# A decoder trunk on one core: the pre-norm gain in x's transposes or in the projection's weights

## The chip, the cores and the metric

The kernel runs on one core of a Trainium2 chip. The metric is the device time of one execution in microseconds (us); a shorter time is better. The kernel before takes 1954.34 us, the median of three runs (1953.93 to 1958.12).

The engines named below: PE is TensorE, DVE is VectorE, ACT is ScalarE, POOL is GpSimd, SP is SyncE, which here issues the loads. Each engine takes its own queue of instructions in order.

## The reference: what is computed

Two decoder layers on x of 256 tokens by 2048 features, float32. Each layer is a normalised attention and a normalised squared-ReLU MLP, with a norm ahead of each and one behind:

```python
def rmsnorm(x, g):
    xf = x.astype(jnp.float32)
    y = xf * lax.rsqrt(jnp.mean(xf * xf, axis=-1, keepdims=True) + RMS_EPS)
    return (y * g.astype(jnp.float32)).astype(x.dtype)

def sq_relu_mlp(x, w_up, w_down):
    h = jax.nn.relu(x @ w_up)
    return (h * h) @ w_down
```

What counts here is `rmsnorm(x, g) @ w`. It is the sum over features k of x[t,k] g[k] w[k,n], times a factor of token t alone, which the kernel applies behind the product. The gain g[k] of a feature may stand with x or with w. Layer 0 has one gain ahead of its query, key and value projections (w_qkv_a); layer 1 has two on the same x, one for the shared keys and values (w_kv_shared) and one for the queries (w_q_b). Each MLP has one, ahead of w_up.

## The kernel before

Features are split into 16 k-blocks of 128, tokens into two halves of 128 (hf). Each product is made from three matmuls, since every float32 operand is held as a rounded part, hi, and the rest, lo: hi by hi, hi by lo, lo by hi.

`weights` makes one weight tile: SP loads 512 KB, which are two k-blocks by 512 columns (raw, three buffers), ACT casts it to hi and DVE subtracts hi from raw to give lo (six buffers each). With a gain it does so per k-block, 128x512 at a time, scaled by a column of gcol (L130 and L131); without one, in one piece of 128x1024 (L124 and L125). gcol holds the gains with features across partitions: `load_gains` brings gains in by a DMA, transposes them on PE (tile gps) and copies them to gcol on DVE (L98), the gain of the first attention first and the other four later.

`to_T` turns x: for a half hf and a group c of four k-blocks, four PE transposes (L184) go to one PSUM bank (pt), one ACT instruction casts the 512 columns to hi (L187), and one DVE instruction gives lo (L188). The tiles are called xa0 (for layer 0's attention; xa00 to xa03 by c), xm0 and xm1 (for the two MLPs) and xa1 (layer 1's attention), each with eight turns, 32 in all.

`head_proj` is the first product on a new turned x: it runs the first half over five weight tiles before the second half is needed (L200 to L202, accumulators kv0 and kv1). It serves the key and value projection of each layer and the first 512 columns of each MLP's w_up. `kv_evac` then brings the keys to SBUF (ktok, L235) and transposes them (pk, L243). `q_proj` makes the queries of one group, between which attention is computed; `up_feat` makes the other 512-column pieces of w_up (L508, L512); `col_pass` runs o_proj and w_down (L200 to L202 too). `add_normed` adds a normed output to x in four pieces of 512 columns (L173) and calls the turn of each piece behind it; with o_proj this is the seam into the MLP, with w_down that into the next layer's attention.

The program is written in the order of the computation. A scheduler of the build lays out each engine's queue before the run, by estimates of its own; at the start, the seams and in attention, instructions of several steps stand mixed on a queue. On the chip an engine waits at the head of its queue until what it needs is there.

## Time and profile before

| | before |
|---|---|
| median of three runs | 1954.34 us |
| the profiled execution | 1956.32 us |
| its span, first to last record | 1954.3 us |
| mean granted clock of PE | 0.997 of full |
| PE busy | 1928.2 us, 99% |
| DVE busy | 1273.6 us, 65% |
| ACT busy | 1097.2 us, 56% |

The durations are those of one profiled execution; 2.0 us of its time lie outside the span. "Busy" is the time that an engine had an instruction under way; matmul ends are modelled, and one instruction's row may run on past the start of the next on the same engine. [...]

### The profile page before, as it was taken

How to read it: one execution, taken by the hardware profiler on the slowest of the kernel's cores; microseconds unless marked ns; L12 is line 12 of the kernel's file. 1: busy time of each engine (PE TensorE's matmuls, PEld its weight loads, DVE VectorE, ACT ScalarE, POOL GpSimd, SP SyncE). 2: the span in 40 equal slices, each digit the busy share in tenths (PEclk: the TensorE clock that was granted, in tenths of full speed). 3: DMA queues.
4: the chain of work that ended last, by engine and by line, in shares of the span. 5: the costliest groups of instructions: out<-in, count | busy, mean ns of one | idle time of the engine just before them, and what ended most of it. 6: DMA issues, size and time to landing. Idle time of an engine off the chain costs nothing.

```text
span 1954.3 us, 28151 instructions
## 1 busy us (share of the span) xinstructions
PE 1928.2 (99%) x10318; PEld 1649.4 (84%) x10318; DVE 1273.6 (65%) x2177; ACT 1097.2 (56%) x1977; POOL 247.1 (13%) x306
## 2 busy tenths in 40 slices
PE   8999999999999999999999999999999999999998
PEld 7998788888888888888789988888888888888886
DVE  6898677546655664675578885775466556656654
ACT  7787566445544553554468874664455345435542
POOL 0242001000100110010202420010011002100111
PEclk9999999999999999999999999999999999999999
DMA  7534657666666666666554346566666666666663
GB/s 228 159 112 141 205 162 214 194 193 188 190 192 190 189 188 192 183 192 196 168 165 150 125 145 199 169 202 198 192 183 194 194 193 185 194 192 187 184 194 128
DMA packets 181642, 354.22 MB, mean 181 GB/s; under 512 B 10912, under 2 KB 11008, under 8 KB 180992
## 3 DMA queue, kind: packets, MB, share of 16 engines
q1 hardware_dynamic: 180736, 348.17, 59.4%
q10 hardware_dynamic: 736, 4.24, 0.6%
q8 instruction: 81, 1.33, 0.3%
q14 instruction: 57, 0.47, 0.1%
q0 software_dynamic: 32, 0.02, 0.0%
HBM read 350.28 MB, written 2.10 MB: 180 GB/s over the span
## 4 chain that ended last, share of the span: by engine, by line
PE 87%; DVE 5%; ACT 5%; DMA 2%; issue 1%; POOL 0%; DVEq 0%; ACTq 0%; SPq 0%
PE u L508 23%; PE o L200 15%; PE o L202 15%; PE o L201 14%; PE u L512 11%; ACT pr L338 1%; DVE lo L131 1%; DVE pr L325 1%; ACT hi L130 1%; PE kv L200 1%; PE kv L201 1%; PE kv L202 1%; PE q L271 1%; PE q L268 1%; PE q L270 1%
## 5 line engine op out<-in xcount | busy, mean ns | idle before, releaser
L131 DVE SCALAR_TENSOR_TENSOR lo<-raw,gcol,hi 128x512 fp32r<-128x512 f32 x672 | 485.9, 753 | 192.3 <-ACT hi L130 181.2
L125 DVE TENSOR_TENSOR lo<-raw,hi 128x1024 fp32r<-128x1024 f32 x320 | 394.5, 1234 | 330.9 <-ACT hi L124 330.3
L508 PE MATMUL u<-xm,hi 128*128 128x512 f32 x1920 | 603.5, 395 | 0.0
L130 ACT ACTIVATE hi<-raw,gcol 128x512 fp32r<-128x512 f32 x672 | 455.0, 716 | 244.4 <-PE u L508 96.3
L124 ACT ACTIVATE hi<-raw 128x1024 fp32r<-128x1024 f32 x320 | 338.9, 1059 | 403.5 <-PE o L202 321.5
L512 PEld LDWEIGHTS u<-xm,lo 128*128 128x128 f32 x1920 | 360.5, 188 | 84.9
L200 PE MATMUL o<-hi,h 128*128 128x512 f32 x1024 | 403.2, 394 | 0.0
L202 PE MATMUL o<-hi,h 128*128 128x512 f32 x1024 | 401.0, 392 | 0.0
L201 PE MATMUL o<-lo,h 128*128 128x512 f32 x1024 | 398.1, 389 | 0.0
L512 PE MATMUL u<-xm,lo 128*128 128x256 f32 x1920 | 377.9, 278 | 0.0
L508 PEld LDWEIGHTS u<-xm,hi 128*128 128x128 f32 x1920 | 293.0, 189 | 0.7
L519 POOL TENSOR_TENSOR us<-us,rb 128x256 f32<-128x256 f32 x120 | 116.0, 967 | 1257.3 <-DVE us L518 1257.3
L202 PEld LDWEIGHTS o<-hi,h 128*128 128x128 f32 x1024 | 192.2, 188 | 44.7
L201 PEld LDWEIGHTS o<-lo,h 128*128 128x128 f32 x1024 | 192.3, 188 | 42.1
L200 PEld LDWEIGHTS o<-hi,h 128*128 128x128 f32 x1024 | 192.5, 188 | 38.8
L268 PE MATMUL q<-xa,hi 128*128 128x256 f32 x512 | 147.0, 287 | 0.0
L271 PE MATMUL q<-xa,lo 128*128 128x256 f32 x512 | 144.8, 283 | 0.0
L270 PE MATMUL q<-xa,hi 128*128 128x256 f32 x512 | 144.4, 282 | 0.0
L521 ACT ACTIVATE h<-uh 128x256 fp32r<-128x256 f32 x120 | 50.2, 419 | 97.1 <-DVE uh L520 97.1
L200 PE MATMUL o<-hi,o 128*128 128x512 f32 x256 | 102.0, 398 | 0.0
L520 DVE SCALAR_TENSOR_TENSOR uh<-us 128x256 f32<-128x256 f32 x120 | 50.8, 423 | 77.5 <-POOL us L519 77.5
L202 PE MATMUL o<-hi,o 128*128 128x512 f32 x256 | 100.8, 394 | 0.4 <-POOL o L378 0.4
(116 smaller groups left out, 1909.3 us busy)
## 6 DMA issues: line engine op xcount, KB each, us to landing
raw<-in_w_up_dram SPq DMA_DIRECT2D x256, 512.0 KB, 4.1
raw<-in_w_down_dram SPq DMA_DIRECT2D x256, 512.0 KB, 4.2
raw<-in_w_qkv_a_dram SPq DMA_DIRECT2D x40, 512.0 KB, 4.1
raw<-in_w_o_a_dram SPq DMA_DIRECT2D x32, 512.0 KB, 4.2
raw<-in_w_q_b_dram SPq DMA_DIRECT2D x32, 512.0 KB, 3.8
raw<-in_w_o_b_dram SPq DMA_DIRECT2D x32, 512.0 KB, 4.1
raw<-in_w_kv_shared_dram SPq DMA_DIRECT2D x8, 512.0 KB, 3.6
x<-in_x_dram SPq DMA_DIRECT2D x8, 256.0 KB, 5.4
```

The source lines that it names most:

```text
L124: nc.scalar.activation(hi, raw, AF.Copy)
L125: nc.vector.tensor_sub(lo, raw, hi.bitcast(F32))
L130: nc.scalar.activation(hi[:, i], raw[:, i], AF.Copy, scale=g)
L131: nc.vector.scalar_tensor_tensor(lo[:, i], raw[:, i], g, hi[:, i].bitcast(F32), op0=ALU.mult, op1=ALU.subtract)
L200: nc.tensor.matmul(ps, xh, wh, start=first, stop=False)
L201: nc.tensor.matmul(ps, xh, wl, start=False, stop=False)
L202: nc.tensor.matmul(ps, xl, wh, start=False, stop=last)
L268: nc.tensor.matmul(o, hi[:, j, fs], t[:, :T], start=(k == 0 and f % 2 == 0), stop=False, skip_group_check=True)
L270: nc.tensor.matmul(o, hi[:, j, fs], t[:, T:], start=False, stop=False, skip_group_check=True)
L271: nc.tensor.matmul(o, lo[:, j, fs], t[:, :T], start=False, stop=(k == KT - 1), skip_group_check=True)
L508: nc.tensor.matmul(acc[f], hi[:, j, fs], xT[k // 4][:, k % 4], start=(k == 0), stop=False, skip_group_check=True)
L512: nc.tensor.matmul(acc[f][:, :T], lo[:, j, fs], xT[k // 4][:, k % 4, :T], start=False, stop=(k == KT - 1), skip_group_check=True)
```

## The change

`to_T` takes the index of a gain. With one, each turn is made in four pieces of 128 columns, one for each k-block: ACT casts a piece with the gain's column of gcol as its scale, and DVE multiplies the piece by the same column and subtracts hi. xa0 (gain 0), xm0 (gain 1) and xm1 (gain 4) have one: 24 of the 32 turns. The weight tiles of w_qkv_a (40) and of w_up (256) then have none and take the plain form of 128x1024; the 40 of w_kv_shared and w_q_b keep theirs, and xa1 is turned as before. Matmuls, loads and transposes are the same in number and shape. Lines behind `to_T` have numbers ten higher after the change.

```diff
-    def to_T(dst, name):
+    def to_T(dst, name, gi=None):
+
 
         def each(hf, c):
             if not dst:
@@ -184,8 +185,17 @@
                 nc.tensor.transpose(pt[:, j * P:(j + 1) * P], xs[hf][:, k * P:(k + 1) * P], ident)
             pt4 = pt.rearrange("p (j t) -> p j t", t=P)
             hi = dst[c][:, :, hf * P:(hf + 1) * P]
-            turned[0] = nc.scalar.activation(hi, pt4, AF.Copy).ins
-            nc.vector.tensor_sub(dst[c][:, :, T + hf * P:T + (hf + 1) * P], pt4, hi.bitcast(F32))
+            lo = dst[c][:, :, T + hf * P:T + (hf + 1) * P]
+            if gi is None:
+                turned[0] = nc.scalar.activation(hi, pt4, AF.Copy).ins
+                nc.vector.tensor_sub(lo, pt4, hi.bitcast(F32))
+                return
+            for j in range(4):
+                k = gi * KT + 4 * c + j
+                g = gcol[:, k:k + 1]
+                turned[0] = nc.scalar.activation(hi[:, j], pt4[:, j], AF.Copy, scale=g).ins
+                nc.vector.scalar_tensor_tensor(lo[:, j], pt4[:, j], g, hi[:, j].bitcast(F32),
+                                               op0=ALU.mult, op1=ALU.subtract)
         return each
 
     def act_tiles(tag, name):
@@ -213,14 +223,14 @@
         n = KT // 2
         head = []
         for i in range(min(STAG, n)):
-            head.append(weights(rows(w, 2 * i, 2, c0, 512), (2, 512), (gi, 2 * i)))
+            head.append(weights(rows(w, 2 * i, 2, c0, 512), (2, 512), gi and (gi, 2 * i)))
             step(0, i, head[i])
             if second and i == X1_AT:
                 second()
         for i, hl in enumerate(head):
             step(1, i, hl)
         for i in range(STAG, n):
-            hl = weights(rows(w, 2 * i, 2, c0, 512), (2, 512), (gi, 2 * i))
+            hl = weights(rows(w, 2 * i, 2, c0, 512), (2, 512), gi and (gi, 2 * i))
             for hf in range(NH):
                 step(hf, i, hl)
         return acc
@@ -257,7 +267,7 @@
 
         acc = [bank("a", f"q{i}") for i in range(2)]
         for i in range(KT // 2):
-            hi, lo = weights(rows(w, 2 * i, 2, g * 512, 512), (2, 512), (gi, 2 * i))
+            hi, lo = weights(rows(w, 2 * i, 2, g * 512, 512), (2, 512), gi and (gi, 2 * i))
             for j in range(2):
                 k = 2 * i + j
                 t = xT[k // 4][:, k % 4]
@@ -500,7 +510,7 @@
 
         acc = [bank(tag, f"u{f}") for f in range(4)]
         for i in range(KT // 2):
-            hi, lo = weights(rows(w, 2 * i, 2, c0, 512), (2, 512), (gi, 2 * i))
+            hi, lo = weights(rows(w, 2 * i, 2, c0, 512), (2, 512), gi and (gi, 2 * i))
             for f in range(4):
                 fs = slice(f * P, (f + 1) * P)
                 for j in range(2):
@@ -535,7 +545,7 @@
 
 
     xT = []
-    turn_x = to_T(xT, "xa0")
+    turn_x = to_T(xT, "xa0", 0)
     for c in range(4):
         turn_x(0, c)
 
@@ -545,7 +555,7 @@
         for c in range(4):
             turn_x(1, c)
 
-    layers = [(w_qkv_a[0], D, 0, w_qkv_a[0], 0, True, near, w_o_a[0]),
+    layers = [(w_qkv_a[0], D, None, w_qkv_a[0], None, True, near, w_o_a[0]),
               (w_kv_shared, 0, 2, w_q_b[0], 3, False, full, w_o_b[0])]
     for layer, (w_kv, c_kv, g_kv, w_q, g_q, with_sink, dist, w_o) in enumerate(layers):
         kv = head_proj(xT, w_kv, c_kv, g_kv, second_half if layer == 0 else None)
@@ -560,9 +570,9 @@
         for g in range(HKV):
             attention(g, q_proj(xT, w_q, g, g_q), ks, vs, oT, dist, with_sink, r, std)
         xT = []
-        o_proj(oT, w_o, n_attn_post[layer], to_T(xT, f"xm{layer}"))
+        o_proj(oT, w_o, n_attn_post[layer], to_T(xT, f"xm{layer}", 1 + 3 * layer))
         xm, xT = xT, []
-        mlp(xm, w_up[layer], w_down[layer], 1 + 3 * layer, n_mlp_post[layer], x_rstd,
+        mlp(xm, w_up[layer], w_down[layer], None, n_mlp_post[layer], x_rstd,
             to_T(xT, "xa1") if layer == 0 else store)
```

The order of the queues comes out another way. At the start on DVE (gcol is the table of gains, gps its transposes in PSUM, lo a weight tile's rest, pt0 to pt3 the turns' banks), before:

```order
L86 MEMSET eps_90 128x1
L98 COPY gcol_92<-gps_95 128x16
L131 SCALAR_TENSOR_TENSOR lo_145<-raw_143,gcol_92,hi_144 128x512
L188 TENSOR_TENSOR xa00_109<-pt0_113,xa00_109 128x4x128
L188 TENSOR_TENSOR xa01_110<-pt1_120,xa01_110 128x4x128
L188 TENSOR_TENSOR xa02_111<-pt2_127,xa02_111 128x4x128
L188 TENSOR_TENSOR xa03_112<-pt3_134,xa03_112 128x4x128
L131 SCALAR_TENSOR_TENSOR lo_145<-raw_143,gcol_92,hi_144 128x512
L131 SCALAR_TENSOR_TENSOR lo_159<-raw_157,gcol_92,hi_158 128x512 x2
```

and after:

```order
L86 MEMSET eps_90 128x1
L125 TENSOR_TENSOR lo_169<-raw_167,hi_168 128x1024
L125 TENSOR_TENSOR lo_181<-raw_179,hi_180 128x1024
L125 TENSOR_TENSOR lo_193<-raw_191,hi_192 128x1024
L98 COPY gcol_92<-gps_95 128x16
L197 SCALAR_TENSOR_TENSOR xa00_109<-pt0_113,gcol_92,xa00_109 128x128
L197 SCALAR_TENSOR_TENSOR xa01_110<-pt1_126,gcol_92,xa01_110 128x128
L197 SCALAR_TENSOR_TENSOR xa02_111<-pt2_139,gcol_92,xa02_111 128x128
L197 SCALAR_TENSOR_TENSOR xa00_109<-pt0_113,gcol_92,xa00_109 128x128
```

The copy of gcol moved from the head of the queue to behind three whole lo tiles, and the pieces of the first three turns stand interleaved behind it. The next lo tile (of lo_269) stands six rows further on, with the fourth piece of xa00 behind it. On ACT the hi casts of the first three tiles stand ahead of the first turn piece in the same way. PE's queue has the first matmul on xa00 behind the sixteen transposes of the first half, as before.

At the seam behind layer 0's o_proj on DVE (x0 is the first half of x, ug1 the output's second half, stat a norm's scalars, xm00 to xm03 the turned x), before:

```order
L173 SCALAR_TENSOR_TENSOR x0_62<-ug0_2186,stat_3051,x0_62 128x512 x4
L188 TENSOR_TENSOR xm00_3060<-pt0_3064,xm00_3060 128x4x128
L188 TENSOR_TENSOR xm01_3061<-pt1_3072,xm01_3061 128x4x128
L188 TENSOR_TENSOR xm02_3062<-pt2_3080,xm02_3062 128x4x128
L188 TENSOR_TENSOR xm03_3063<-pt3_3088,xm03_3063 128x4x128
L432 TENSOR_TENSOR ug1_2187<-o11_2786,grow_2184 128x512
L142 TENSOR_REDUCE stat_3131<-parts_2189 128x1
L131 SCALAR_TENSOR_TENSOR lo_3227<-raw_3225,gcol_92,hi_3226 128x512
L145 TENSOR_SCALAR stat_3131<-stat_3131 128x1
L131 SCALAR_TENSOR_TENSOR lo_3227<-raw_3225,gcol_92,hi_3226 128x512
L131 SCALAR_TENSOR_TENSOR lo_3241<-raw_3239,gcol_92,hi_3240 128x512 x2
```

and after, from the last instruction on ug1 (ahead of it stand the lo of the first four weight tiles, the four adds to x0, and the first pieces of xm00 and xm01):

```order
L442 TENSOR_TENSOR ug1_2155<-o11_2754,grow_2152 128x512
L197 SCALAR_TENSOR_TENSOR xm00_3028<-pt0_3032,gcol_92,xm00_3028 128x128
L197 SCALAR_TENSOR_TENSOR xm01_3029<-pt1_3046,gcol_92,xm01_3029 128x128
L197 SCALAR_TENSOR_TENSOR xm02_3030<-pt2_3060,gcol_92,xm02_3030 128x128
L197 SCALAR_TENSOR_TENSOR xm03_3031<-pt3_3074,gcol_92,xm03_3031 128x128
L142 TENSOR_REDUCE stat_3123<-parts_2157 128x1
L125 TENSOR_TENSOR lo_3249<-raw_3247,hi_3248 128x1024
L145 TENSOR_SCALAR stat_3123<-stat_3123 128x1
L125 TENSOR_TENSOR lo_3291<-raw_3289,hi_3290 128x1024
L197 SCALAR_TENSOR_TENSOR xm00_3028<-pt0_3032,gcol_92,xm00_3028 128x128
```

The lo of weight tile 4 moved to ahead of the adds, and the lo of tiles 5 and 6 (lo_3249, lo_3291) moved to between the second and the third piece of xm00. The fourth piece of xm00 stands four rows further on.

At the same place on ACT (o11 is an accumulator of o_proj, hi a weight tile's cast), before:

```order
L153 ACTIVATE junk_3128,parts_2189<-o11_2786 128x512
L187 ACTIVATE xm00_3060<-pt0_3064 128x4x128
L187 ACTIVATE xm01_3061<-pt1_3072 128x4x128
L130 ACTIVATE hi_3240<-raw_3239,gcol_92 128x512
L187 ACTIVATE xm02_3062<-pt2_3080 128x4x128
L187 ACTIVATE xm03_3063<-pt3_3088 128x4x128
L130 ACTIVATE hi_3240<-raw_3239,gcol_92 128x512
L130 ACTIVATE hi_3284<-raw_3283,gcol_92 128x512 x2
```

and after:

```order
L153 ACTIVATE junk_3120,parts_2157<-o11_2754 128x512
L124 ACTIVATE hi_3248<-raw_3247 128x1024
L196 ACTIVATE xm00_3028<-pt0_3032,gcol_92 128x128
L196 ACTIVATE xm01_3029<-pt1_3046,gcol_92 128x128
L124 ACTIVATE hi_3290<-raw_3289 128x1024
L196 ACTIVATE xm00_3028<-pt0_3032,gcol_92 128x128
L196 ACTIVATE xm01_3029<-pt1_3046,gcol_92 128x128
L196 ACTIVATE xm02_3030<-pt2_3060,gcol_92 128x128
L196 ACTIVATE xm03_3031<-pt3_3074,gcol_92 128x128
L536 DMA grow_3187<-in_norm_mlp_post_dram 128x2048
L196 ACTIVATE xm00_3028<-pt0_3032,gcol_92 128x128
```

The hi of tile 5 (hi_3248), ahead of whose first half two turns stood, moved to ahead of the first piece, and that of tile 6 to behind the first two. Layer 1's seam has the same order on both engines.

## Rows read from the trace of the kernel before

**Rows 1.** The page: busy time by engine, and the chain that ended last.
```profile
PE 1928.2 (99%) x10318; PEld 1649.4 (84%) x10318; DVE 1273.6 (65%) x2177; ACT 1097.2 (56%) x1977; POOL 247.1 (13%) x306
...
PE 87%; DVE 5%; ACT 5%; DMA 2%; issue 1%; POOL 0%; DVEq 0%; ACTq 0%; SPq 0%
```

**Rows 2.** Stretches: length, busy us of PE, PEld, DVE, ACT, POOL, clock, DMA.
```profile
40.00:210.00 170.00, 166.76 (x1186) 153.96 (x1185) 146.71 (x377) 134.65 (x337) 48.66 (x75) 1.00 0.47 145
262.00:270.00 8.00, 7.93 (x43) 6.34 (x42) 7.98 (x15) 5.66 (x12) 0.00 (x0) 1.00 0.51 156
320.00:640.00 320.00, 320.00 (x1597) 270.08 (x1596) 186.56 (x256) 158.79 (x229) 24.23 (x26) 1.00 0.65 192
...
1600.00:1900.00 300.00, 300.00 (x1544) 254.95 (x1544) 184.72 (x271) 151.02 (x230) 31.47 (x33) 1.00 0.64 190
```

**Rows 3.** The page's groups of instructions: count | busy, mean ns | idle before.
```profile
L131 DVE SCALAR_TENSOR_TENSOR lo<-raw,gcol,hi 128x512 fp32r<-128x512 f32 x672 | 485.9, 753 | 192.3 <-ACT hi L130 181.2
L125 DVE TENSOR_TENSOR lo<-raw,hi 128x1024 fp32r<-128x1024 f32 x320 | 394.5, 1234 | 330.9 <-ACT hi L124 330.3
...
L130 ACT ACTIVATE hi<-raw,gcol 128x512 fp32r<-128x512 f32 x672 | 455.0, 716 | 244.4 <-PE u L508 96.3
L124 ACT ACTIVATE hi<-raw 128x1024 fp32r<-128x1024 f32 x320 | 338.9, 1059 | 403.5 <-PE o L202 321.5
```

**Rows 4.** Groups by line and form over the span: the rows nearest to the new pieces.
```profile
L188 DVE TENSOR_TENSOR xm<-pt,xm 128x512 fp32r<-128x512 f32 x16 | 10.6, 688 | 0.3
...
L187 ACT ACTIVATE xa<-pt 128x512 fp32r<-128x512 f32 x16 | 9.1, 596 | 10.2 <-PE pt L184 9.9
...
L345 ACT ACTIVATE pr<-pr,st 128x128 f32<-128x128 f32 x16 | 5.5, 390 | 0.8 <-DVE st L341 0.8
...
L239 DVE SCALAR_TENSOR_TENSOR vs<-kv,stat,vs 128x256 fp32r<-128x256 f32 x4 | 1.9, 474 | 0.0
...
L238 ACT ACTIVATE vs<-kv,stat 128x256 fp32r<-128x256 f32 x4 | 1.9, 465 | 0.0
```

**Rows 5.** Timelines of the start, ACT, DVE, PE: start us, busy us, engine, line, operation.
```profile
8.63 0.72 ACT L130 ACTIVATE hi<-raw,gcol 128x512 fp32r<-128x512 f32 x1 [6.61 <-DMA raw<-in_w_qkv_a_dram]
9.26 2.04 ACT L187 ACTIVATE xa<-pt 128x512 fp32r<-128x512 f32 x4
...
10.06 2.48 DVE L188 TENSOR_TENSOR xa<-pt,xa 128x512 fp32r<-128x512 f32 x4
...
9.89 0.50 PE L200 MATMUL kv<-hi,xa 128*128 128x512 f32 x1 [2.05 <-ACT xa L187]
...
13.87 1.85 PE L184 MATMUL pt<-ident,x 128*128 128x128 f32 x8
...
17.37 0.39 PE L200 MATMUL kv<-hi,xa 128*128 128x512 f32 x1
```

**Rows 6.** Busy time by stretch, as rows 2: the start, and the turn into xa1.
```profile
8.00:10.00 2.00, 0.11 (x1) 0.11 (x1) 0.61 (x1) 1.37 (x3) 0.00 (x0) 1.00 1.01 369
...
12.00:14.00 2.00, 1.45 (x6) 1.30 (x7) 2.00 (x4) 2.00 (x4) 0.00 (x0) 0.53 0.72 276
14.00:16.00 2.00, 2.00 (x11) 1.93 (x10) 2.00 (x5) 1.68 (x4) 0.00 (x0) 0.62 0.77 216
...
974.00:980.00 6.00, 4.53 (x25) 3.38 (x25) 6.00 (x10) 3.36 (x7) 1.70 (x1) 1.00 0.63 162
```

**Rows 7.** Timelines of the seam behind layer 0's o_proj: DVE, ACT, PE.
```profile
261.55 2.74 DVE L173 SCALAR_TENSOR_TENSOR x<-ug,stat,x 128x512 f32<-128x512 f32 x4
...
264.27 0.72 ACT L130 ACTIVATE hi<-raw,gcol 128x512 fp32r<-128x512 f32 x1
...
264.15 0.48 PE L200 MATMUL kv<-hi,xm 128*128 128x512 f32 x1
...
267.42 0.39 PE L200 MATMUL kv<-hi,xm 128*128 128x512 f32 x1
```

**Rows 8.** Timeline of PE behind the first head projection.
```profile
39.12 0.44 PE L243 MATMUL pk<-ident,ktok 128*128 128x128 f32 x2 [0.91 <-ACT ktok L235]
```

## The prediction

> **What bounds the kernel now.** I read the page's busy shares first: TensorE (PE) is busy 99% of the span, VectorE (DVE) 65%, ScalarE (ACT) 56%, and PE carries 87% of the chain that ended last [rows 1]. So work taken off DVE or ACT pays only where PE waits for them. Next I read the busy time by stretch of the span. In the long MLP stretches PE is busy for every microsecond (320 to 640 and 1600 to 1900 are shown; 640 to 960 and 1290 to 1600 read the same), with DVE and ACT at about six and five tenths; in layer 0's attention, 40 to 210, PE is idle for 170 - 166.76 = 3.2 us and DVE is at 147 of 170 [rows 2]. Last I read the engines' timelines at the two kinds of place where the new instructions go: the start [rows 5] and the stretch behind o_proj [rows 7].
>
> **What the change removes.** 296 weight tiles (40 of w_qkv_a, 256 of w_up) go from two scaled 512-column pieces on each engine to one plain 1024-column piece. Means are 716 and 753 ns for the pieces, 1059 and 1234 ns for the whole [rows 3]. Instructions of one queue overlap a little: four casts of 596 ns stand in 2.04 us, so the next starts after 0.48, and four subtractions of 688 ns in 2.48 us give 0.60 [rows 4, 5]. Taking about 0.10 off each mean, a tile costs ACT 0.96 where it cost 1.24, and DVE 1.14 where it cost 1.32: savings of 0.28 and 0.18 us. For the 256 tiles of w_up this is worth nothing, since PE never waits in those stretches [rows 2]; if PE were not the cover there, it would be at most 256 x 0.28 = 72 us. For the 32 q tiles in attention it is 9.0 us of ACT and 5.8 of DVE beside PE's 3.2 us of idle [rows 2]. That idle sits in many short waits behind chains of several instructions, and the order on the queues is new as well, so I take -2, with bounds -6 (as much again may lie under the modelled ends of matmul rows) and +2.
>
> **What it adds.** 24 turns of x go from one instruction on each engine to four of 128 columns, scaled by a column of gcol. No row shows that form. On DVE the nearest row is 474 ns (256 columns from PSUM, scaled by a column), 0.38 us of the queue: half of that, 0.19, would be 128 columns with no fixed part; with the 688 ns of 512 columns the line through both gives 370 ns, 0.28 of the queue. I take 0.25, nearer to the line. On ACT 390 ns (128 scaled from SBUF) and 465 ns (256 from PSUM) give 0.28 [rows 4]. A turn then costs DVE 1.0 us for 0.60, and ACT 1.1 for 0.48. [...]
>
> All four pieces of one turn read one PSUM bank, and in the new order ACT's second piece stands behind DVE's first, so the two engines alternate. With 24 x 0.4 to 0.6 us the added work alone is about 10 to 15 us, of which only what lies on the way to PE's next matmul counts.
>
> **The start.** Now the first weight tile's load is down by 8.63, its first half is cast, the four turns follow, and PE's first matmul on them starts at 9.89; the fifth k-block starts at 17.37 [rows 5]. The weights need no gcol any more, and the new order puts three whole lo tiles ahead of the copy of gcol on DVE. The third tile needs two more loads of 512 KB at 369 GB/s, 1.4 us each [rows 6]: down at 11.4, cast by 12.5, its lo by 13.8, gcol at 13.9, the first scaled piece at 14.3. PE's first matmul moves from 9.89 to about 14.35. Behind it DVE has nine pieces (2.3 us), a lo tile (1.14) and one piece before k-block 3 is whole: 17.9 with no wait between the engines, 18.8 if each piece waits for the other engine's as the order says; I take 18.8, so k-block 4 starts at 19.1, 1.7 later than now. Before 17.37, PE had also done 12 transposes of the second half (the last eight from 13.87 [rows 5]) and the second gains' (1.6 us at the full clock), which are now still to come. That makes 3.4. Against it stands the 0.91 us that PE waits at 39.12 for ktok [rows 8]: those transposes now stand six matmuls further back, so I count -0.9. The start costs +2.5, with bounds +1 and +4.
>
> The clock adds to that. [...] In the new order PE lies still until 14.35, 4.5 us longer. [...] I count +1 (0 to +3.4, twice that loss).
>
> **The two seams behind o_proj.** In both layers this is the same code. Now: four adds to x from 261.55, PE's first matmul on the turned x at 264.15, k-block 4 at 267.42 [rows 7]. The new order moves the lo of tile 4 ahead of the adds (they move to about 262.7), puts the hi of tile 5, whose load is down at 264.27 [rows 7], whole (0.96) ahead of the first scaled cast, and puts the lo of tiles 5 and 6 (2 x 1.14) between the second and the third piece of xm00 (k-blocks 0 to 3, a piece each). So: hi of tile 5 to 265.2, first piece 265.5, PE's first matmul there instead of 264.15. On DVE: first piece 265.8, fourth add 266.4, xm01 266.65, ug 267.25, four pieces 268.3, reduce, two lo tiles 270.8, then xm00's third piece 271.0 and, four pieces on, its fourth at 272.0. PE needs these in order for the last product of k-blocks 2 and 3: k-block 4 starts at 272.3 instead of 267.42, +4.9. Some of it comes back, since the second half's adds have more time: I take +4.3 a seam, 2.5 to 5.5, so +8.6 for both. The turn into xa1 is unchanged and counts nothing. SP's loads wait for a raw buffer (three of them), which a lo sets free; the lo tiles of the seams come earlier or at the same place, so I count nothing for the loads; a load that did come late would add its 1.4 us [rows 6].
>
> **The sum.** Start +2.5, clock +1, seams +8.6, attention -2: +10.1. The profiled execution took 1956.32 us for a span of 1954.3, so 1966.4 in its terms; it lies 1.98 above the median of the runs (1954.34), and on that scale the forecast is 1964.4 us.
>
> **Rivals.**
> (a) The waits are mostly covered. If the load of tile 5 is down before the adds end, or PE's queue runs the second half's transposes meanwhile, a seam costs 1 us instead of 4.3, the start 2: 2 + 2 - 2 = +2, 1956.3. For it speaks that the seam is now covered whole, PE idle for 0.07 of the 8 us from 262 to 270 [rows 2]; against it, that DVE takes its queue in order, holds two lo tiles ahead of the pieces PE needs, and is itself busy 7.98 of those 8 us, with no slack to give.
> (b) Faster. The lighter casts dissolve the waits in layer 0's attention. Mechanism: there DVE works 147 of 170 us, ACT 135 [rows 2], and q tiles pass through both just ahead of PE. At the bound of -6, with seams at 0 and the start at +1, it is -5, 1949.3. It decides from the point where the attention gain exceeds start and seams together, which needs DVE to be done with xm00 before 267.4; the order puts about 3 us of lo in front of that.
> (c) The clock falls at the seams too. PE would have 16 transposes and 12 products, some 4.5 us of work, in the ten from 262.4 to 272.3, and at the start the clock fell after a thin stretch [rows 6]. If each seam runs 3.4 us at the half rate, that is 1.7 more each, and with the full 3.4 at the start and seams at 5.5: 3.4 + 2.5 + 2 x (5.5 + 1.7) - 2 = +18.3, 1972.6. Against it: from 974 to 980, at the turn into xa1, PE is busy 4.53 of 6 us and the clock stays at 1.00 [rows 6], and a thinner stretch at a seam is not in this trace. [...]
>
> **How the numbers follow.** Forecast (its own range +5 to +14, 1959.3 to 1968.3): 0.63. (a): 0.15. (b): 0.06. (c): 0.16. A measurement of this kernel can tell about 0.2%, 3.9 us. The range reaches over (a)'s middle at the low end, 1956.5, and into (c) at the high end, 1971.5, leaving out (b), half of (a) and a third of (c), under 2 in 10. Slower by over 0.2%: forecast and (c), 0.79; within: (a), 0.15; faster: (b), 0.06.
>
> **What would show it.** In the trace after: PE's first kv matmul near 14.3 and the clock at half until 17 or later; at both seams two lo tiles on DVE between the pieces of xm00, and PE waiting 1 to 3 us at a time for the subtraction of the turn; MLP stretches at 100% as now, with ACT and DVE lighter by 0.28 and 0.18 us a tile; pieces of 128 columns at some 0.25 to 0.28 us apart. I am wrong if a piece takes 0.2 us or less, if PE shows under 1 us of waits at the seams, or if attention shortens by more than 4 us.

## The result

The changed kernel takes 1967.83 us (median of four runs, 1966.03 to 1968.98) where the kernel before takes 1954.71; the ratio is 1.0060, with a 95% interval of 1.0048 to 1.0073. Run again beside the last experiments it took 1967.94 us, ratio 1.0062 (1.0049 to 1.0074). It is slower by about 0.6%, 12 to 13 us by the medians.

The profiled execution of the change took 1966.03 us for a span of 1964.2; beside [rows 1] its page reads:

```profile
PE 1930.6 (98%) x10318; PEld 1651.5 (84%) x10318; DVE 1213.9 (62%) x1953; ACT 1034.6 (53%) x1753; POOL 226.9 (12%) x306
...
PE 88%; DVE 6%; ACT 3%; issue 1%; DMA 1%; SPq 0%; DVEq 0%; ACTq 0%
```

DVE has lost 60 us of work and ACT 63, and the span is 9.9 us longer. The next view is that of the change's groups by line and form, the rows of the two new pieces and of the plain weight tile:

```profile
L125 DVE TENSOR_TENSOR lo<-raw,hi 128x1024 fp32r<-128x1024 f32 x616 | 755.9, 1228 | 543.9 <-ACT hi L124 541.8 <-PE u L518 0.3
...
L196 ACT ACTIVATE xm<-pt,gcol 128x128 fp32r<-128x128 f32 x64 | 19.3, 368 | 15.3 <-PE pt L185 8.1 <-DVE xm L197 6.8
L197 DVE SCALAR_TENSOR_TENSOR xm<-pt,gcol,xm 128x128 fp32r<-128x128 f32 x64 | 18.7, 344 | 6.6 <-ACT xm L196 6.5
```

What PE waited for in the change (us in total, times, longest), the largest four:

```profile
PE pt L185 <- DVE gcol L98: 6.7, 1, 6.7
PE kv L212 <- DVE xm L197: 4.1, 2, 2.0
PE pt L185 <- DVE x L173: 3.3, 4, 1.5
PE kv L210 <- ACT xm L196: 2.6, 2, 1.3
```

The first of these is the start. The second and fourth are the seams, once each per layer; none of the three existed before. The third did exist: 1.7 of its 3.3 us are the turn into xa1, the rest are two new waits of 0.8 at the seams.

Busy time by stretch in the change (columns as in rows 2), to be read beside [rows 2, 6]:

```profile
12.00:14.00 2.00, 0.46 (x2) 0.46 (x3) 1.36 (x4) 0.56 (x3) 0.00 (x0) 0.50 1.01 378
14.00:16.00 2.00, 2.00 (x8) 1.71 (x7) 1.77 (x7) 2.00 (x8) 0.00 (x0) 0.50 1.03 336
16.00:18.00 2.00, 2.00 (x6) 1.52 (x6) 1.67 (x4) 2.00 (x7) 0.00 (x0) 0.50 0.62 228
18.00:20.00 2.00, 2.00 (x10) 1.55 (x9) 2.00 (x6) 2.00 (x4) 0.00 (x0) 0.96 0.27 41
40.00:210.00 170.00, 168.39 (x1204) 156.78 (x1203) 144.07 (x356) 128.02 (x314) 54.82 (x76) 1.00 0.50 153
262.00:270.00 8.00, 4.72 (x24) 3.01 (x24) 6.71 (x15) 5.39 (x14) 0.00 (x0) 1.00 0.74 264
266.00:268.00 2.00, 0.90 (x3) 0.48 (x3) 0.92 (x4) 2.00 (x7) 0.00 (x0) 1.00 0.61 204
268.00:270.00 2.00, 0.80 (x3) 0.30 (x2) 2.00 (x5) 0.85 (x4) 0.00 (x0) 1.00 0.81 332
270.00:272.00 2.00, 1.09 (x3) 0.88 (x4) 2.00 (x7) 1.11 (x5) 0.00 (x0) 0.69 0.68 147
272.00:274.00 2.00, 2.00 (x6) 1.59 (x5) 1.91 (x9) 1.04 (x5) 0.00 (x0) 0.50 0.95 350
...
320.00:640.00 320.00, 320.00 (x1598) 270.05 (x1597) 174.07 (x207) 145.67 (x179) 20.01 (x27) 1.00 0.64 191
```

In the MLP PE is busy for all of the 320 us as before, with DVE 12 us lighter for nothing. Attention's idle time is down from 3.2 to 1.6 us. PE is idle for 3.3 of the 8 us of the seam, where it was for 0.07, and the granted clock, 1.00 at full, stands at 0.50 from 270.75 to 274.2 (below: half rate).

The stages of each run's trace, in us, tell where the time went. "Start" is the time of the first matmul of q; "att 0" from there to the last matmul on po; "seam 0" from there to the first matmul on u (it holds o_proj, the turn and the first projection); "att 1" from the first matmul on kv in layer 1 to the last on po; "seam 1" as seam 0. The MLP stretches (from the first matmul on u to the first on kv in layer 1, and to the last matmul of all) are 690 and 687 us in all of them, within 1 us. The medians and ratios are of the timed runs.

| run | start | att 0 | seam 0 | att 1 | seam 1 | median | ratio, interval |
|---|---|---|---|---|---|---|---|
| before | 37.0 | 166.3 | 85.7 | 193.6 | 84.4 | 1954.7 to 1956.4 | 1 |
| the change | 40.4 | 163.3 | 90.7 | 191.9 | 90.6 | 1967.8 | 1.0060 (1.0048 to 1.0073) |
| change_again | 40.9 | 163.3 | 91.3 | 193.4 | 91.5 | 1967.9 | 1.0062 (1.0049 to 1.0074) |
| xa0_only | 40.8 | 163.3 | 85.2 | 192.0 | 84.4 | 1956.1 | 1.0003 (0.9994 to 1.0011) |
| xm_only | 38.1 | 166.8 | 91.4 | 193.4 | 91.3 | 1968.3 | 1.0064 (1.0050 to 1.0078) |
| weights_only | 42.0 | 163.3 | 86.7 | 193.6 | 86.0 | 1959.0 | 1.0014 (1.0005 to 1.0023) |
| turns_only | 37.7 | 168.3 | 89.5 | 193.3 | 88.5 | 1963.4 | 1.0041 (1.0027 to 1.0054) |
| act_first | 43.8 | 164.6 | 85.8 | 192.5 | 85.2 | 1959.4 | 1.0019 (1.0010 to 1.0028) |
| seam_lo | 40.4 | 163.3 | 87.8 | 193.7 | 86.9 | 1961.6 | 1.0024 (1.0014 to 1.0034) |
| seam_warm | 41.0 | 163.3 | 91.2 | 193.4 | 90.9 | 1967.0 | 1.0051 (1.0038 to 1.0065) |
| weights_start | 40.6 | 163.8 | 87.3 | 192.3 | 85.9 | 1955.5 | 0.9997 (0.9988 to 1.0006) |
| xa0_act_start | 40.8 | 165.9 | 85.3 | 192.0 | 84.4 | 1954.8 | 0.9994 (0.9985 to 1.0003) |
| before_warm | 39.5 | 167.6 | 85.3 | 192.4 | 84.4 | 1957.6 | 1.0013 (1.0004 to 1.0022) |
| xa0_act_warm | 40.0 | 164.0 | 85.4 | 192.2 | 84.4 | 1954.6 | 0.9992 (0.9983 to 1.0000) |

Layer 1's attention is the same code in all of them and reads 191.9 to 193.7: that is how far one execution differs from the next there. Six of the seven executions at 193.3 to 193.7, that of before among them, had one or two loads of 5.6 to 6.4 us from issue to landing in the stage's first 50 us, and none of the seven at 191.9 to 192.5 had one there; so the change's 1.7 us in that stage is taken for late loads in the trace of before, and no gain of the change. The profiled execution of the change is also the fastest of its four; change_again's span, 1967.7, lies nearer to the medians.

The columns of the seams hold o_proj too. In layer 0 its last matmul stands 57.9 to 58.9 us behind the last one on po, and two traces of the same kernel (the change, change_again) read 57.9 and 58.8; so that 1 us is no effect of the edits. These rows are the last matmul of o_proj and the last of the first projection at layer 0's seam, first before, then in the change:

```profile
262.21 0.39 PE L202 MATMUL o<-hi,o 128*128 128x512 f32 x1
...
288.68 0.39 PE L202 MATMUL kv<-hi,xm 128*128 128x512 f32 x1
...
261.53 0.39 PE L212 MATMUL o<-hi,o 128*128 128x512 f32 x1
...
294.09 0.39 PE L212 MATMUL kv<-hi,xm 128*128 128x512 f32 x1
```

From the one to the other (below: "from o_proj's end"), seam 0 and seam 1 take, in us:

| run | seam 0 | seam 1 |
|---|---|---|
| before | 26.5 | 26.5 |
| the change | 32.6 | 32.6 |
| change_again | 32.2 | 33.6 |
| xm_only | 32.4 | 33.3 |
| seam_warm | 32.1 | 32.1 |
| turns_only | 30.6 | 30.6 |
| seam_lo | 29.2 | 29.0 |
| weights_only | 27.3 | 27.3 |
| act_first | 27.3 | 27.3 |

By this measure the change costs 5.8 to 7.1 us a seam.

### The profile page after: what moved, and what is told of

Same layout as the page of the kernel before. It is cut to its first block, busy times and chain, and to the rows that moved or that the text cites. A ratio compares the mean times of both kernels' runs of the same rounds, so it can differ in the third digit from the quotient of the medians.

```text
span 1964.2 us, 27669 instructions
## 1 busy us (share of the span) xinstructions
PE 1930.6 (98%) x10318; PEld 1651.5 (84%) x10318; DVE 1213.9 (62%) x1953; ACT 1034.6 (53%) x1753; POOL 226.9 (12%) x306
## 4 chain that ended last, share of the span: by engine, by line
PE 88%; DVE 6%; ACT 3%; issue 1%; DMA 1%; SPq 0%; DVEq 0%; ACTq 0%
PE u L518 23%; PE o L210 15%; PE o L212 15%; PE o L211 14%; PE u L522 11%; PE kv L212 1%; ACT pr L348 1%; PE kv L210 1%; PE kv L211 1%; DVE pr L335 1%; PE q L280 1%; PE q L278 1%; PE q L281 1%; DVE lo L125 1%; DVE pr L357 1%
## 5 line engine op out<-in xcount | busy, mean ns | idle before, releaser
L125 DVE TENSOR_TENSOR lo<-raw,hi 128x1024 fp32r<-128x1024 f32 x616 | 755.9, 1228 | 543.9 <-ACT hi L124 541.8
L124 ACT ACTIVATE hi<-raw 128x1024 fp32r<-128x1024 f32 x616 | 651.9, 1059 | 708.0 <-PE o L212 384.5
L529 POOL TENSOR_TENSOR us<-us,rb 128x256 f32<-128x256 f32 x120 | 88.9, 741 | 1298.0 <-DVE us L528 1298.0
L212 PEld LDWEIGHTS o<-hi,h 128*128 128x128 f32 x1024 | 192.2, 188 | 44.7
L211 PEld LDWEIGHTS o<-lo,h 128*128 128x128 f32 x1024 | 192.3, 188 | 42.1
L210 PEld LDWEIGHTS o<-hi,h 128*128 128x128 f32 x1024 | 192.5, 188 | 38.8
L211 PE MATMUL o<-lo,o 128*128 128x512 f32 x256 | 100.9, 394 | 0.0
L280 PEld LDWEIGHTS q<-xa,hi 128*128 128x128 f32 x512 | 97.7, 191 | 0.8
L278 PEld LDWEIGHTS q<-xa,hi 128*128 128x128 f32 x512 | 97.6, 191 | 0.7
```

What stands on the lines that cost most here:

```text
L124: nc.scalar.activation(hi, raw, AF.Copy)
L125: nc.vector.tensor_sub(lo, raw, hi.bitcast(F32))
L210: nc.tensor.matmul(ps, xh, wh, start=first, stop=False)
L211: nc.tensor.matmul(ps, xh, wl, start=False, stop=False)
L212: nc.tensor.matmul(ps, xl, wh, start=False, stop=last)
L278: nc.tensor.matmul(o, hi[:, j, fs], t[:, :T], start=(k == 0 and f % 2 == 0), stop=False, skip_group_check=True)
```

## The experiments

**The two halves of the edit.** `weights_only` takes the gain from the weights and leaves the turns as they were; `turns_only` makes the turns in pieces and leaves the weights as they were. So the first leaves three gains out of the computation, and the second applies them twice. (In `turns_only`, and in `xm_only` below, `gi and (gi, 2 * i)` also becomes `None if gi is None else (gi, 2 * i)` at the four calls of `weights`, since the first gain's index is 0; these lines are not shown here.)

```diff
 weights_only (against the change)
-    turn_x = to_T(xT, "xa0", 0)
+    turn_x = to_T(xT, "xa0")
...
-        o_proj(oT, w_o, n_attn_post[layer], to_T(xT, f"xm{layer}", 1 + 3 * layer))
+        o_proj(oT, w_o, n_attn_post[layer], to_T(xT, f"xm{layer}"))
 turns_only (against the change)
...
-    layers = [(w_qkv_a[0], D, None, w_qkv_a[0], None, True, near, w_o_a[0]),
+    layers = [(w_qkv_a[0], D, 0, w_qkv_a[0], 0, True, near, w_o_a[0]),
...
-        mlp(xm, w_up[layer], w_down[layer], None, n_mlp_post[layer], x_rstd,
+        mlp(xm, w_up[layer], w_down[layer], 1 + 3 * layer, n_mlp_post[layer], x_rstd,
```

> The 296 weight tiles lose the gain as in the change, the turns stay one instruction on each engine (so the gain of three norms is left out of the computation). My theory, that the seams' loss is the scaled pieces alternating between ACT and DVE with two lo tiles among them: both seams within 1 us of before, layer 0's attention 3 us shorter as in the changed kernel, and a start that still loses about 2 us because three lo tiles stay ahead of the gains' copy and the turns. Total 1952 to 1955, against 1967.8 of the change. Rival, that the whole 128x1024 forms on the queues ahead of the turn do it: seams of +4 to +5 each, total 1963 or more.

> The turns are made in four scaled pieces as in the change, and the weight tiles keep their gain and their two 512-column pieces (so three gains are applied twice). My theory: both seams lose about 5 us, first matmul at the start is near before since the gains' copy is first on DVE again, start +1 to +2, layer 0's attention no shorter; total 1965 to 1967. Rival, that the weights' forms are the cause: 1955 to 1957.

Measured: 1958.96 and 1963.41 us. Both totals miss their ranges, the first from above, the second from below. The seams of `weights_only` are near before: 86.7 and 86.0, in which the first matmul on u stands 0.8 us later and the MLP behind it is as much shorter (689.3 for 690.1); from o_proj's end they are 0.8 us longer than before. Attention is 2.9 shorter as expected; but the start is 42.0, 4.9 later than before, with no piece in it. The run's PE timeline shows why:

```profile
13.76 1.11 PE L185 MATMUL pt<-ident,x 128*128 128x128 f32 x4 [6.60 <-DVE gcol L98]
...
14.52 0.77 PE L210 MATMUL kv<-hi,xa 128*128 128x512 f32 x1
```

The fourth turn's transposes wait for the copy of gcol, which no turn reads here. The gains' transposes (gps) hold one of the four PSUM banks of that pool until DVE has copied them, and DVE has three lo tiles ahead of the copy. In the change it is the same wait, 6.7 us. In all seven kernels that have this copy behind three lo tiles, with pieces or without, PE's first matmul on xa00 starts 3.24 to 3.25 us after the third weight tile has landed (11.28 and 14.52 here, 11.06 and 14.31 in the change). `turns_only`, where the copy is first on DVE, starts at 37.7. Its seams are 89.5 and 88.5, 3.8 and 4.1 over before, with 168.3 in attention for 166.3: the rival, 1955 to 1957, is out. From o_proj's end its seams cost 4.1 us each where those of `weights_only` cost 0.8 and the change's 6.1; so most of the seams' loss comes with the turns, and some 1.2 us only with both halves together. Why attention took 168.3 is not shown.

**The two places.** `xa0_only` moves the gain of the first attention alone, `xm_only` those of the MLPs alone.

```diff
 xa0_only (against the change)
-        o_proj(oT, w_o, n_attn_post[layer], to_T(xT, f"xm{layer}", 1 + 3 * layer))
+        o_proj(oT, w_o, n_attn_post[layer], to_T(xT, f"xm{layer}"))
-        mlp(xm, w_up[layer], w_down[layer], None, n_mlp_post[layer], x_rstd,
+        mlp(xm, w_up[layer], w_down[layer], 1 + 3 * layer, n_mlp_post[layer], x_rstd,
 xm_only (against the change)
...
-    turn_x = to_T(xT, "xa0", 0)
+    turn_x = to_T(xT, "xa0")
...
-    layers = [(w_qkv_a[0], D, None, w_qkv_a[0], None, True, near, w_o_a[0]),
+    layers = [(w_qkv_a[0], D, 0, w_qkv_a[0], 0, True, near, w_o_a[0]),
```

> Only the first attention's gain moves into x's turns (xa0, 40 tiles of w_qkv_a); both MLP gains stay in w_up. Start +3.3 and layer 0's attention -3.0 as in the changed kernel, both seams as before: total 1954 to 1956. If the gain in attention was not from the lighter q tiles but from the phase of the loads, it would not be there again and the total is 1957 to 1959. In layer 1's attention, whose code is the same, the changed kernel's trace was 1.7 us shorter; if that was a late load in the one execution of before, this run's differs too, without a pattern.

> Only the two MLP gains move into x's turns; the first attention's stays in its weights. If the parts add, the start and layer 0's attention are as before and each seam costs 5.2: total 10 us over before, 1965 to 1967. If the seams' loss in the change depended on what came ahead of them, under 1962.

Measured: 1956.09 us, the same as before (ratio 1.0003), and 1968.33. In `xa0_only` the start's +3.8 and attention's -3.0 cancel, and the seams are as before. `xm_only` misses its range: it is 12.4 over the kernel before that ran beside it, not 10, with seams of 91.4 and 91.3, +5.8 and +6.9. The parts add: 0.1 and 12.4 against 12.0 of the change in that company.

**The seams' order.** `act_first` keeps the 24 turns in four pieces and writes the four casts ahead of the four subtractions:

```diff
+            g = [gcol[:, gi * KT + 4 * c + j:gi * KT + 4 * c + j + 1] for j in range(4)]
             for j in range(4):
-                k = gi * KT + 4 * c + j
-                g = gcol[:, k:k + 1]
-                turned[0] = nc.scalar.activation(hi[:, j], pt4[:, j], AF.Copy, scale=g).ins
-                nc.vector.scalar_tensor_tensor(lo[:, j], pt4[:, j], g, hi[:, j].bitcast(F32),
-                                               op0=ALU.mult, op1=ALU.subtract)
+                turned[0] = nc.scalar.activation(hi[:, j], pt4[:, j], AF.Copy, scale=g[j]).ins
+            for j in range(4):
+                nc.vector.scalar_tensor_tensor(lo[:, j], pt4[:, j], g[j], hi[:, j].bitcast(F32),
+                                               op0=ALU.mult, op1=ALU.subtract)
```

> The change with one edit: the four scaled casts of a turn are written ahead of its four subtractions, so that each engine has its four pieces in a row and the lo tiles of the seam come behind them. Same number of pieces. My theory (alternation and the lo tiles among the pieces, not the number of pieces): PE's 2.0 us waits for the subtraction at the seams go and a seam costs 0.5 to 2 us; start still +3, layer 0's attention -3; total 1955 to 1959. Rival, that four pieces instead of one are the cost by themselves: seams still +4 to +5, total 1964 to 1967.

Measured: 1959.36 us, just over the range, with seams of 85.8 and 85.2, within 0.8 of before. DVE at its seam:

```profile
266.92 2.74 DVE L173 SCALAR_TENSOR_TENSOR x<-ug,stat,x 128x512 f32<-128x512 f32 x4
269.57 0.69 DVE L442 TENSOR_TENSOR ug<-o,grow 128x512 f32<-128x512 f32 x1
270.17 4.22 DVE L197 SCALAR_TENSOR_TENSOR xm<-pt,gcol,xm 128x128 fp32r<-128x128 f32 x16
274.31 0.15 DVE L142 TENSOR_REDUCE stat<-parts 128x1 f32<-128x4 f32 x1
274.37 1.22 DVE L125 TENSOR_TENSOR lo<-raw,hi 128x1024 fp32r<-128x1024 f32 x1
```

Sixteen pieces stand in a row in 4.22 us, 0.258 each ((4.22 - 0.344) / 15), and no lo tile among them; PE takes them as they come: behind 0.82 us for the adds its timeline shows no wait from 269.06 to 275. From o_proj's end both seams are 0.8 us longer than before, as in `weights_only`, which has no piece. So the four pieces as such cost the seam nothing. At the start this run is worse than the change (43.8), in an execution whose first weight tile was down only at 10.9 us, where it was at 8.1 in the change (the third at 13.6, for 11.1); PE waited 9.2 us for the copy of gcol there.

`seam_lo` keeps the alternation and moves only the lo of tiles 5 and 6 on DVE, behind the last piece of xm01:

```diff
+            with tc.issue_after(piece[0]) if i == 4 and piece[0] else nullcontext():
+                head.append(weights(rows(w, 2 * i, 2, c0, 512), (2, 512), gi and (gi, 2 * i)))
-            head.append(weights(rows(w, 2 * i, 2, c0, 512), (2, 512), gi and (gi, 2 * i)))
```

(and the same for i == 5; piece[0] is the last subtraction of xm01's first half).

> The change with one edit at both seams: the lo of weight tiles 5 and 6 is queued on DVE behind the last piece of xm01 instead of between the second and third pieces of xm00; the pieces still alternate between ACT and DVE. My theory (two lo tiles, 2.3 us, ahead of the piece that PE waits for): PE's 2.0 us wait for the subtraction goes, the clock stays up, k-block 4 starts near 270 instead of 272.8, a seam costs 2 to 3 us instead of 5.2; total 1961 to 1964 against 1967.8. Rival, that the alternation alone holds PE: waits stay, 1966 or more.

Measured: 1961.62 us, seams of 87.8 and 86.9: 2.9 and 3.7 us less than the change's. Its PE has the wait for the cast left, and none for the subtraction:

```profile
263.29 1.29 PE L186 MATMUL pt<-ident,x 128*128 128x128 f32 x8 [0.82 <-DVE x L174]
...
267.48 0.50 PE L213 MATMUL kv<-hi,xm 128*128 128x512 f32 x1 [1.19 <-ACT xm L197]
...
270.52 0.40 PE L213 MATMUL kv<-hi,xm 128*128 128x512 f32 x1
```

The last row is k-block 4. From o_proj's end its seams are 3.4 and 3.6 us shorter than the change's and 2.7 and 2.5 longer than before. So of the 6 us of a seam the two lo tiles among the pieces are some 3.5, what the half rate costs behind them included. Of the rest 0.82 is the wait behind the adds, which have a lo tile ahead of them now, and 1.2 the wait for ACT's second piece, behind tile 6's cast; the share of the alternation itself is not separated.

**The clock.** `seam_warm` is the change with 28 transposes of no use on PE at each seam (the calls, 12 and 16 at a time, are not shown here).

```diff
+    def busy(ps, n, behind):
+        for i in range(n):
+            with tc.issue_after(behind):
+                behind = mm_ins(nc.tensor.transpose(ps[:, :P], ident, ident))
+        return behind
```

> The change with 28 idle transposes on PE at each seam, 12 ahead of the first matmul on the turned x and 16 ahead of the one that waits longest (they write a bank that is overwritten later); no queue but PE's changes. In the change's trace seven to ten matmuls behind that wait start 0.43 us apart instead of 0.23. If the clock falls because PE lies still, it stays at full here and each seam is 1.6 to 2 us shorter: 1963.5 to 1965. If the slow matmuls only fill time in which PE would wait anyhow, or PE loses as much to the transposes: 1967 or more.

Measured: 1966.98 us, seams of 91.2 and 90.9. The clock did stay at full, 1.00:

```profile
268.00:270.00 2.00, 2.00 (x14) 1.50 (x13) 2.00 (x7) 1.20 (x5) 0.00 (x0) 1.00 0.97 401
270.00:272.00 2.00, 1.70 (x11) 1.21 (x10) 2.00 (x6) 0.76 (x3) 0.00 (x0) 1.00 0.56 131
272.00:274.00 2.00, 1.96 (x8) 1.05 (x6) 1.91 (x10) 1.39 (x6) 0.00 (x0) 1.00 1.03 374
274.00:276.00 2.00, 1.23 (x10) 1.15 (x10) 2.00 (x4) 0.37 (x1) 0.00 (x0) 1.00 0.14 52
```

and PE waits instead, at 274.77, for the second half's adds to x on DVE, which is busy through all of it:

```profile
274.77 0.66 PE L185 MATMUL pt<-ident,x 128*128 128x128 f32 x4 [0.82 <-DVE x L173]
```

The rival holds in the main, with the total just at its edge: in the change the slow matmuls mostly fill time in which PE would wait for DVE. They do not do so wholly. From o_proj's end both seams of `seam_warm` take 32.1 us (its columns above hold 0.8 us by which the first matmul on u stands later, as in `weights_only`). The four traced seams of the change, change_again and `xm_only` that lost 1.7 us of clock take 32.2 to 32.6, and the two that lost 3.4 us take 33.3 and 33.6. So by this run half rate cost 0.1 to 0.6 us where 1.7 were lost and 1.2 to 1.5 where 3.4 were, and more if the transposes of no use cost time themselves, which no run separates. In the timed runs `seam_warm` is 10.6 us over the kernel before beside it and the change 12.0; the intervals of the two ratios overlap.

**The start.** `xa0_act_start` and `weights_start` put the first gains' copy ahead of the lo tiles on DVE and the first half's turn ahead of the second and third casts on ACT, on top of `xa0_only` with `act_first`'s order and of `weights_only` (so `weights_start` leaves three gains out too):

```diff
-            nc.scalar.activation(hi, raw, AF.Copy)
-            nc.vector.tensor_sub(lo, raw, hi.bitcast(F32))
+            made[0] += 1
+            with tc.issue_after(turned[0] if made[0] in (2, 3) else copied[0]):
+                nc.scalar.activation(hi, raw, AF.Copy)
+            with tc.issue_after(copied[0]):
+                nc.vector.tensor_sub(lo, raw, hi.bitcast(F32))
```

> Only the first attention's gain in x's turns, the four casts of a turn written ahead of its four subtractions, and the start put in another order: the gains' copy first on DVE, the turn's pieces behind the first weight tile and ahead of the casts of the second and third. If the start's loss in the change is the order (gains' copy behind three lo tiles, the fourth turn's PSUM bank held until then), the start is within 1 us of before, layer 0's attention keeps its -3.0, the seams are as before: 1952 to 1954, under both kernels. If the four pieces by themselves cost the start, +3 stays there and the total is 1955 to 1957.

> The weight tiles without the gain and turns of one instruction (three gains are left out), as in the earlier run of that kind, with the same order at the start as the run above. That earlier run lost 5.0 us at the start with no piece in it at all. If that was the gains' copy holding a bank behind three lo tiles, it goes: start within 1 us of before, total 1952.5 to 1954.5. If the plain 128x1024 first tile is the cost (a whole tile cast ahead of the turn instead of half of one), +2 or more stays: 1956 or more.

Measured: 1954.81 and 1955.51 us, 1.3 under `xa0_only` and 3.5 under `weights_only`, and no different from before (ratios 0.9994 and 0.9997). Each lies between the two cases that were expected. The long wait for gcol is gone and PE's first matmul on xa00 comes at 12.0 and 11.0, in executions whose first weight tile was down only at 10.6 and 9.4. Both profiled executions are slower than their medians (1957.66 and 1957.52), and the start they show is still 3.5 to 3.8 over that of before, of which the later tile may be 0.8 to 2.1. Both also ran at half rate for 6.8 us there, where before did for 3.4. What holds the rest is not settled.

`before_warm` and `xa0_act_warm` put 38 transposes of no use at the start, into the kernel before and into `xa0_act_start`, made by the same `busy`:

```diff
+        b = busy(spare, 20, turn_pe[0]) if spare is not None else None
+        for a, w, s, e in ((xh, wh, first, False), (xh, wl, False, False), (xl, wh, False, last)):
+            with tc.issue_after(b) if b else nullcontext():
+                m = nc.tensor.matmul(ps, a, w, start=s, stop=e)
+            if spare is not None:
+                b = busy(spare, 6, mm_ins(m))
```

> The kernel before with 38 idle transposes on PE at the start, 20 ahead of the first matmul on the turned x and six behind each of the first three. In the trace of before PE ran 3.4 us at half rate there, 1.7 us of clock. If that is lost time, the clock stays up and the total is 1 to 2 us lower, 1953.5 to 1955; if DVE and ACT set the pace of the start whatever the clock, as at the seams, within 0.5 us of before.

> The first attention's gain in x's turns with the start in the other order, as run above (1954.8), and the same idle transposes at the start. That run's trace had 6.8 us at half rate, 3.4 us of clock, where before had 1.7. If that is lost time: 2 to 3 us lower, 1951.5 to 1953; if not, 1954 to 1955.5.

Measured: 1957.56 and 1954.64 us. The clock was at full, 1.00, from beginning to end of both starts. The first is 1.6 us slower than before, which neither of its cases has. The extra transposes also put PE's queue in another order (the second half's transposes stand later), and in its trace 3.4 us at half rate come right behind the start instead, from 41.2, so this run does not tell what the half rate costs. The second is level with the run without them, whose trace has 6.8 us at half rate in the start and 3.4 more from 43.2: there a clock held up gave nothing back that the timed runs show. `xa0_act_warm`, the lowest ratio of all (0.9992, interval to 1.0000), is within what can be told from the kernel before; no version was found that is clearly faster.

**Once more.**

> The change itself once more, beside these runs, for a second trace and more timed runs: 1966 to 1968.5, clock lost 1.7 us at each seam and 3.4 at the start, first matmul on the turned x near 14.3 if the first weight tile is down near 8.1 and later by as much as the tile is.

Measured: 1967.94 us, clock lost 1.7 us at seam 0 as expected and 3.4 at seam 1, where half rate lasted from 1245 to 1251; first matmul at 14.5, 0.2 later than in the first trace, as the third tile was (11.3); the first, at 8.6, was 0.45 later.

## Why the prediction came out

The forecast was 1964.4 us, range 1956.5 to 1971.5, slower with 0.79; measured 1967.8. The sign and the places are right, and the sum of +10.1 stands against +9.7 for the two profiled executions but 12 to 13 for the medians. That it lies so near to 9.7 is luck: the trace of before was 1.7 us longer in layer 1's attention and 1.0 in o_proj, which no edit touched, and the seams lost more than forecast. By its own terms:

- **MLP, 0.** Right. 690.15 us from seam to turn before, 690.13 after.
- **Attention, -2.** Measured -3.0, in every run with plain q tiles and in its usual order (163.3 six times, for 166.3), within the bounds of -6 and +2. The four other runs with plain q tiles read 163.8 to 165.9, the four with the gain in them 166.3 to 168.3; in the traces of `xa0_act_start` (165.9) and `before_warm` (167.6) half rate stood in this stage.
- **The pieces, 0.25 and 0.28 us.** Measured 0.258 on DVE (above) and, from eight of 368 ns in 2.16 us on ACT, 0.256. The author's estimates from the rows of larger forms [rows 4] were 0.01 too low on DVE and 0.02 too high on ACT. That the pieces are small did not cost the seams: `act_first` has all of them, and from o_proj's end its seams lose no more than those of `weights_only`, which has none (0.8 us each).
- **The start, +2.5 and +1 for the clock.** Measured +3.3 and +3.9 in the two traces, so the two terms together are right (1.7 and 1.6 make 3.3, not 3.4: a tenth). The first matmul came at 14.31 for a forecast of 14.35, by the third weight tile's landing, three lo tiles and the copy of gcol as worked out, but partly for another reason behind the copy. I had the scaled pieces wait for gcol; PE's transposes of the fourth turn wait for it as well, by the PSUM bank, and `weights_only` shows that this alone does it. k-block 4 came at 18.96 for 19.1. The clock lost 3.4 us (0.50 from 11.3 to 18.2) for 1.7 before (2 x 0.47 + 2 x 0.38 from 12 to 16 [rows 6], as 3.4 us at half rate would). The +1, and the 3.4 us that (c) counts for the start, are the author's estimates beside that loss of 1.7, the second twice the loss. No run shows them: none held the clock at this start, and `xa0_act_warm` shows no gain from holding it at another (1954.64 us for 1954.81).
- **The seams, +4.3 each.** This is the term that was mis-sized. By the columns it is +5.1 and +6.2 in the first trace, +5.7 and +7.1 in the second, and from o_proj's end +6.1 and +6.2, +5.8 and +7.1: 12 to 13 us where I had 8.6. The mechanism is the one described. DVE and PE at the seam of the change:

```profile
268.19 1.21 DVE L125 TENSOR_TENSOR lo<-raw,hi 128x1024 fp32r<-128x1024 f32 x1
269.32 0.14 DVE L145 TENSOR_SCALAR stat<-stat 128x1 f32<-128x1 f32 x1
269.38 1.21 DVE L125 TENSOR_TENSOR lo<-raw,hi 128x1024 fp32r<-128x1024 f32 x1
270.51 2.15 DVE L197 SCALAR_TENSOR_TENSOR xm<-pt,gcol,xm 128x128 fp32r<-128x128 f32 x8
...
268.47 0.40 PE L211 MATMUL kv<-lo,xm 128*128 128x512 f32 x1
270.91 0.80 PE L212 MATMUL kv<-hi,xm 128*128 128x512 f32 x1 [2.05 <-DVE xm L197]
...
272.79 0.63 PE L210 MATMUL kv<-hi,xm 128*128 128x512 f32 x1
```

The third piece starts at 270.51 (forecast 271.0 less a piece) behind the two lo tiles, and k-block 4 at 272.79 (272.3). But o_proj had ended 0.7 us earlier here than before. From its end k-block 4 is 6.0 us behind before, where the forecast has 4.9: the third piece came 0.4 us later than worked out, and from it to k-block 4 PE ran at half rate, which the term held at nothing; in `seam_warm`, at full clock, k-block 4 is 5.2 behind. And the sentence that some of the 4.9 comes back failed: the first projection's end is 6.1 behind. The second half's adds and sixteen pieces queue on DVE right behind the first half's, so there is nothing that catches up; `seam_warm` shows PE meeting them (0.82 us at 274.77). A small miss within it: the load of tile 5 was down earlier than in the trace of before (cast from 262.58, not 264.27), and PE's first matmul on xm00 came at 263.95, not 265.5; it was the load of tile 6 that ACT then waited for, 1.29 us, with the second pieces of xm00 and xm01 behind it. The hand-off moved by one tile and the sum hardly at all.

- **The rivals.** (a), covered waits, did not happen in the change, but it is what `act_first` does: idle at the seam falls to the 0.8 us behind the adds. Its total stays 3.4 us over the kernel before beside it, with its start at 43.8. (b) did not come: the gain in attention stayed at 3.0. (c) was half right: the clock did fall at both seams, losing 1.7 us each in the first trace, as it said, after PE had been busy 0.90 and 0.80 us of the 2 from 266 and from 268; its price was too high, since DVE's queue was behind it most of the time. Where 1.7 us were lost a seam was 0.1 to 0.6 us longer than in `seam_warm`, and where half rate lasted twice as long (seam 1 of change_again and of `xm_only`, 3.4 us lost) 1.2 to 1.5.

## What to carry to other kernels

When work is taken off engines that are not the bound, look first at whether the bound engine waits for them anywhere; 256 of these 296 tiles could give nothing, and 24 turns could lose. A change of form is also a change of order: splitting one instruction into pieces written alternately on two engines that share a PSUM bank let other work in between them, and writing each engine's pieces in a row took all but 0.8 us of a loss of 6 to 7 us a seam away. And when a copy out of PSUM slides back in its queue, look at who needs its bank, not only at who reads its result: in `weights_only` PE waited 6.60 us for a copy that no turn read.

## What the runs showed that was not expected

- The first weight tile was down between 8.0 and 10.9 us from one execution to another, with the same queue of loads. In the change's order it is the third tile, down between 11.1 and 13.6, that sets the first matmul, 3.2 us later.
- PE ran at half rate at the seams of the change, and with the clock held at full by transposes of no use its seams ended 0.1 to 1.5 us sooner, less than half of the 1.7 to 3.4 us of clock that were lost.
- One or two loads of about 6 us where most take 4 go, in six traces of seven, with 1.4 to 1.8 us more in layer 1's attention, as much as some of the kernels here differ by.
